# Second feed-forward stage: TensorE's steps of the state-space preparation one group later; output matrices signed on GpSimd

## The chip, the cores and the metric

One core of a Trainium2 chip runs the whole program, two transformer blocks over 256 tokens of width 1024, in one launch. The metric is the device time of that launch in microseconds, the median of several runs. Lower is better.

## The reference, cut to what matters

The change lies where the first block's second feed-forward stage runs and the second block's state-space mixer is prepared:

```python
x = x + 0.5 * _swiglu(_rms_norm(x, ffn2_norm), ffn2_w1, ffn2_w3, ffn2_w2)   # D_FF = 2816
...
dt = exp(log_dt);  mag = exp(lam_re * dt);  ang = lam_im * dt
lb = mag * (cos(ang) + i sin(ang))          # 32 groups x 64 complex states
f  = (lb - 1) / lam;  bb = f * b            # input matrices
bu = einsum('bsgh,gph->sbgp', u, bb)
st = associative_scan(st[t] = lb * st[t-1] + bu[t])
y  = Re(c) . Re(st) - Im(c) . Im(st) + d_skip * u
```

The kernel works the scan in chunks of four tokens. For that it needs, from the parameters alone: powers of `lb` (`pw`), the input matrices times these powers (`ws`), their transposes (`bx`), the products of `c` with them for the tokens inside a chunk (`kt`), `c` times the powers with a sign on the imaginary half (`cy`), and tables of `exp(i ang t)` (`E`) and of decays (`R4`). None of it depends on the tokens, so it is computed beside the second feed-forward stage.

## The kernel before

The two feed-forward stages are one function, `ffn` (L418). It runs over 11 groups of 256 hidden units. For each group it takes four weight blocks of 512 KB from a stream (`W.next()`), makes 2 x 48 matmuls `hT` (three for each product, for the high and low parts of both sides), a SiLU and a product on ScalarE and VectorE, and then `second`, 24 matmuls `yacc` with two more weight blocks for the group before. Each weight block `w` is split by `wsplit` (L294): ScalarE writes the high part `whi` (L301), VectorE the low part `wlo` (L316; the first of a stage at L308, one of them on GpSimd). `whi` and `wlo` have four buffers each.

`s5_prep` (L806) returns the preparation as steps for `ffn`'s `hooks`: a step of group g is written out ahead of that group's own work. `params` (group 0) and `powers` (1) make the small tables in `s5z`; `inputs` (2) makes `ws` on GpSimd, four rounds of six operations of 128x512 and eight copies; `kernels(o)` (groups 4 to 7, o = 0 to 3) has the TensorE step: eight transposes `bxp` (L896) and eight small products `k` (L350) that read `ws[o]`, then two ScalarE copies to `bx` (L897) and ten to `kt` (L907). `kernels(0)` also clears the two halves of `kt` on GpSimd (L890, L891). `outputs` (8) makes the four `cy` from products `ctmp` on GpSimd, 24 operations, and four sign changes on VectorE (L919). `tables` (9) makes `E` and `R4`.

Nothing runs in the order in which it is written. A scheduler takes the instructions by priority, the earlier written ahead of the later, as their inputs and buffers come free by its own estimate of times, and fixes one order for each engine; on the chip each engine then works its list strictly in order and waits by semaphores. `after(i, j)` (L322) orders i behind j on that list; `pinned` (L339) keeps a chain of matmuls in the order written, in stages where it is on (it is off in the feed-forward stages). Buffers: `Q` has 9 slots of 512 columns, which the SiLU results also use; `M` has two tags, `m` with 6 slots (`wide=False`: `bc`, `kt`, two of the `cy`) and `r3` with 13 (`wide=True`).

Of the kernel before, what the change touches and what calls it, by code (L numbers as in the profile page):

```python
# [12 lines left out]
OP = mybir.AluOpType  # L13
# [36 lines left out]
def transformer_kernel(ctx: ExitStack, tc: tile.TileContext, A, out, stop=None):  # L50
# [50 lines left out]
    def Q(shape, dt=F32, name="q"):  # L101
        return tl(qpool, "q", 512, shape, dt, name)
# [234 lines left out]
    def pinned(i):  # L337

        if "pin" in cur:  # L339
            if cur["pin"] is not None:  # L340
                after(i, cur["pin"])
            cur["pin"] = i

    def mm3(o, lh, ll, rh, rl, start, stop):
        pinned(PE.matmul(o, lh, rh, start=start, stop=False))  # L345
        pinned(PE.matmul(o, lh, rl, start=False, stop=False))  # L346
        pinned(PE.matmul(o, ll, rh, start=False, stop=stop))  # L347

    def mm(o, l, r, start=True, stop=True, **kw):
        pinned(PE.matmul(o, l, r, start=start, stop=stop, **kw))  # L350
# [454 lines left out]

    def s5_prep(pr):  # L806

        z = M([28, 16], name="s5z", wide=True)
        lre, lim = vec[:, V_LRE:V_LRE + 16], vec[:, V_LIM:V_LIM + 16]
        dt, mag, ang, sn, cs, half = (z[:, n, :] for n in range(6))  # L810
        t = [z[:, n, :] for n in range(6, 10)]
# [2 lines left out]
        pw[0] = (lbr, lbi)  # L814
        r4 = z[:, 23, :]
        un = [(z[:, 24, :], z[:, 25, :]), (z[:, 26, :], z[:, 27, :])]

        def bcast(q):
            return q[:, :, None].to_broadcast([P, 16, 32])
# [37 lines left out]
        def powers():  # L857
            cmul(*pw[1], lbr, lbi, lbr, lbi, t, G)
            cmul(*pw[2], *pw[1], lbr, lbi, t, G)
            cmul(*pw[3], *pw[1], *pw[1], t, G)  # L860
            G.tensor_tensor(r4, mag, mag, op=OP.mult)
            G.tensor_tensor(r4, r4, r4, op=OP.mult)
            cmul(*un[0], cs, sn, cs, sn, t, G)
            cmul(*un[1], *un[0], *un[0], t, G)

        def inputs():

            pr["ws"] = [M([2, 4, 4, 32], name="ws", wide=True) for _ in range(4)]
            b = pr["bc"][0]
            for n in range(4):  # L870
                tmp = [Q([16, 32], name="wtmp") for _ in range(2)]
                cur_ = H([2, 16, 32], name="wcur")
                cur_ = [cur_[:, 0], cur_[:, 1]]
                if n == 0:
                    cmul(cur_[0], cur_[1], b[:, 0], b[:, 1], bcast(fr), bcast(fi), tmp, G)
                else:
                    cmul(cur_[0], cur_[1], last[0], last[1], bcast(lbr), bcast(lbi), tmp, G)
                for o in range(4):
                    for ri in range(2):
                        G.tensor_copy(pr["ws"][o][:, ri, :, 3 - n, :], cur_[ri][:, 4 * o:4 * o + 4, :])  # L880
                last = cur_

        def kernels(o):
            def f():
                if o == 0:
                    pr["cim"] = Q([16, 32], name="cim")
                    V.tensor_scalar(pr["cim"], pr["bc"][1][:, 1], -1.0, None, op0=OP.mult)
                    pr["bx"] = [M([2, 4, P], name="bx", wide=True) for _ in range(4)]
                    pr["kt"] = [M([16, 2, 32], name="kt", wide=False) for _ in range(2)]
                    G.memset(pr["kt"][0], 0.0)  # L890
                    G.memset(pr["kt"][1], 0.0)  # L891
                wp = pr["ws"][o].rearrange("p r t j h -> p r t (j h)")
                for ri in range(2):
                    p = PT([4, P], name="bxp")
                    for i in range(4):
                        PE.transpose(p[:, i, :], wp[:, ri, i, :], ident)  # L896
                    S.copy(pr["bx"][o][:, ri], p)  # L897
                pk = PT([4, 32], name="k")
                for i in range(4):
                    tt = 4 * o + i  # L900
                    mm(pk[:, i, :], wp[:, 0, i, :], pr["bc"][1][:, 0, tt, :], start=True, stop=False)
                    mm(pk[:, i, :], wp[:, 1, i, :], pr["cim"][:, tt, :], start=False, stop=True)

                for j in range(4):
                    for jj in range(j + 1):
                        src = 3 - (j - jj)
                        S.copy(pr["kt"][j // 2][jj * 32:(jj + 1) * 32, 4 * o:4 * o + 4, j % 2, :],  # L907
                               pk[src * 32:(src + 1) * 32, :, :])
            return f

        def outputs():
            pr["cy"] = [M([2, 16, 32], name="cy", wide=n < 2) for n in range(4)]
            c = pr["bc"][1]
            for n in range(4):
                tmp = M([2, 16, 32], name="ctmp", wide=True)
                tmp = [tmp[:, 0], tmp[:, 1]]
                cy = pr["cy"][n]
                cmul(cy[:, 0], cy[:, 1], c[:, 0], c[:, 1], bcast(pw[n][0]), bcast(pw[n][1]), tmp, G)
                V.tensor_scalar(cy[:, 1], cy[:, 1], -1.0, None, op0=OP.mult)  # L919

        def tables():

# [6 lines left out]
            for k in range(6):  # L929
# [9 lines left out]
            V.tensor_copy(R4, r4[:, :, None].to_broadcast([P, 16, 64]))  # L939
            V.memset(R4[:, :, 0:1], 0.0)  # L940

        return {0: [params], 1: [powers], 2: [inputs], 4: [kernels(0)], 5: [kernels(1)], 6: [kernels(2)],
                7: [kernels(3)], 8: [outputs], 9: [tables]}

    def s5_pool(x, pr, before):
        for i in range(2):
# [806 lines left out]
```

## Time and profile before

| | |
|---|---|
| median of 3 runs | 1308.74 us (1304.94 to 1309.45) |
| the profiled execution | 1304.89 us |
| its span, first to last instruction | 1302.7 us |
| TensorE (PE) busy | 1241.5 us, 95% |
| VectorE (DVE), ScalarE (ACT), GpSimd (POOL) busy | 607.7, 514.9, 269.3 us |
| mean granted clock of TensorE | 0.972 of full speed |
| second feed-forward stage | about 339 to 545 us |

The profile is one execution. Its parts used here: the busy time of the engines; the same in stretches of the span, with the clock that TensorE was granted (1.00 is 2.4 GHz, 0.50 is 1.2 GHz); each engine's instructions in order of time, with the idle time before one in brackets and what ended it; and the instructions on one tile. Times are microseconds from the start of the span. A TensorE row's duration is that of a pipelined matmul; the distance between two starts is what one costs.

### The profile page before, as it was taken

Reading aid. Unit: us, or ns where it says so; the run is one execution under the profiler, and the core shown is the slowest. Engines: PE = TensorE matmul, PEld = TensorE weight load, DVE = VectorE, ACT = ScalarE, POOL = GpSimd, SP = SyncE. Lnnn points to the kernel's source line nnn. Section 1 sums busy time; section 2 is a strip of 40 time slices with the busy share of each in tenths; the row PEclk is TensorE's granted clock in tenths of the full one; section 3 lists DMA queues with packets and bytes.
Section 4 is the critical chain, followed back from the end, with each engine's and each line's share of the span. In section 5 each row is a group of like instructions: output and inputs, shape, how many; then the busy total and the mean of one; then the engine's idle time right before and its main releaser. Section 6 shows DMA issues by size and latency. Waiting matters only on the chain. (4 is left out here: it accounts for less than half of the span.)

```text
span 1302.7 us, 19644 instructions
## 1 busy us (share of the span) xinstructions
PE 1241.5 (95%) x7726; PEld 906.6 (70%) x7726; DVE 607.7 (47%) x975; ACT 514.9 (40%) x774; POOL 269.3 (21%) x318
## 2 busy tenths in 40 slices
PE   8999999999999999998999997997999999997996
PEld 7999997887898999897635453445988734454433
DVE  6445548886664645477512123115755514114113
ACT  5444445575444554435421131114677422122111
POOL 4000001002499547213101220002311101220001
PEclk9999999999898999999999998998999899998998
DMA  9765565435454556536899997999835698998995
GB/s 342 232 188 184 181 191 178 131 130 169 138 179 128 176 152 199 165 128 229 325 395 384 386 385 276 395 398 369 329 112 180 218 373 302 383 389 311 358 393 216
DMA packets 175273, 335.36 MB, mean 257 GB/s; under 512 B 10337, under 2 KB 72305, under 8 KB 175170
## 3 DMA queue, kind: packets, MB, share of 16 engines
q1 hardware_dynamic: 173696, 330.34, 71.8%
q0 software_dynamic: 896, 2.98, 0.6%
q8 instruction: 64, 1.05, 0.3%
q10 hardware_dynamic: 578, 0.67, 0.2%
q14 instruction: 39, 0.32, 0.1%
HBM read 332.91 MB, written 1.05 MB: 256 GB/s over the span
## 5 line engine op out<-in xcount | busy, mean ns | idle before, releaser
L316 DVE TENSOR_TENSOR wlo<-w,whi 128x1024 fp32r<-128x1024 f32 x200 | 266.2, 1338 | 208.5 <-ACT whi L301 205.8
L301 ACT ACTIVATE whi<-w 128x1024 fp32r<-128x1024 f32 x234 | 246.4, 1059 | 247.3 <-PE hT L346 118.8
L350 PE MATMUL h<-w,xg 128*64 128x512 f32 x1024 | 225.6, 594 | 0.5
L345 PE MATMUL hT<-xTh,whi 128*128 128x256 f32 x704 | 202.1, 287 | 0.1
L346 PE MATMUL hT<-xTl,whi 128*128 128x256 f32 x704 | 201.3, 286 | 0.4 <-DVE xTl L334 0.3
L347 PE MATMUL hT<-xTh,wlo 128*128 128x256 f32 x704 | 200.8, 286 | 0.0
L350 PEld LDWEIGHTS h<-w,xg 128*64 128x64 f32 x1024 | 72.3, 137 | 137.8 <-issue 132.1
L345 PEld LDWEIGHTS hT<-xTh,whi 128*128 128x128 f32 x704 | 137.3, 195 | 1.5 <-ACT xTh L332 0.5
L346 PEld LDWEIGHTS hT<-xTl,whi 128*128 128x128 f32 x704 | 137.1, 195 | 1.4 <-DVE xTl L334 0.8
L347 PEld LDWEIGHTS hT<-xTh,wlo 128*128 128x128 f32 x704 | 136.9, 195 | 0.0
L350 PE MATMUL ey<-w,ehTs 128*64 128x512 f32 x512 | 114.2, 593 | 0.4
L335 DVE SCALAR_TENSOR_TENSOR yl<-ey,sgate,yh 128x512 fp32r<-128x512 f32 x32 | 24.0, 749 | 180.1 <-ACT yh L332 179.0
L332 ACT ACTIVATE yh<-ey,sgate 128x512 fp32r<-128x512 f32 x32 | 22.0, 688 | 167.6 <-PE ey L350 127.3
L350 PEld LDWEIGHTS ey<-w,ehTs 128*64 128x64 f32 x512 | 38.6, 137 | 70.8 <-issue 62.8
L316 POOL TENSOR_TENSOR wlo<-w,whi 128x1024 fp32r<-128x1024 f32 x16 | 37.7, 2382 | 222.2 <-ACT whi L301 142.4
L345 PE MATMUL tr<-xTh,whi 128*128 128x256 f32 x256 | 73.9, 289 | 0.4 <-ACT xTh L332 0.4
L346 PE MATMUL tr<-xTl,whi 128*128 128x256 f32 x256 | 73.2, 286 | 0.3 <-DVE xTl L334 0.3
L347 PE MATMUL tr<-xTh,wlo 128*128 128x256 f32 x256 | 72.6, 284 | 0.0
L346 PE MATMUL yacc<-wlo,hh 128*128 128x512 f32 x176 | 68.7, 391 | 0.0
L345 PE MATMUL yacc<-whi,hh 128*128 128x512 f32 x176 | 68.7, 390 | 0.0
L347 PE MATMUL yacc<-whi,hl 128*128 128x512 f32 x176 | 68.6, 390 | 0.0
L357 POOL TENSOR_TENSOR brs<-rp,cm 128x1 f32<-128x1 f32 x8 | 4.4, 550 | 299.3 <-DVE rp L356 297.4
(444 smaller groups left out, 2138.1 us busy)
## 6 DMA issues: line engine op xcount, KB each, us to landing
w<-in_moe_w SPq DMA_DIRECT2D x384, 512.0 KB, 10.2
w<-in_ffn_w SPq DMA_DIRECT2D x132, 512.0 KB, 4.3
w<-in_w_in SPq DMA_DIRECT2D x28, 512.0 KB, 3.9
w<-in_sb_qkv SPq DMA_DIRECT2D x24, 512.0 KB, 10.5
w<-in_ple_gate SPq DMA_DIRECT2D x16, 512.0 KB, 9.0
w<-in_w_out SPq DMA_DIRECT2D x8, 512.0 KB, 3.2
w<-in_ab_w_in SPq DMA_DIRECT2D x8, 512.0 KB, 4.4
w<-in_ab_w_out SPq DMA_DIRECT2D x8, 512.0 KB, 4.1
```

Of the source, the lines that this page charges most:

```text
L301: a = S.activation(hi, t, AF.Copy)
L316: i = eng.tensor_tensor(lo, t, fb(hi), op=OP.subtract)
L332: cur["act"] = S.activation(hi, src, AF.Copy if isinstance(scale, float) else AF.Identity, scale=scale)
L335: return V.scalar_tensor_tensor(lo, src, scale, fb(hi), op0=OP.mult, op1=OP.subtract)
L345: pinned(PE.matmul(o, lh, rh, start=start, stop=False))
L346: pinned(PE.matmul(o, lh, rl, start=False, stop=False))
L347: pinned(PE.matmul(o, ll, rh, start=False, stop=stop))
L350: pinned(PE.matmul(o, l, r, start=start, stop=stop, **kw))
L357: cur["pow"] = G.tensor_tensor(o, t, cm05[:, :n], op=OP.pow)
```

## The change

Four edits, all in the preparation:

- The hook table: `kernels(0)` to `kernels(3)` go from groups 4 to 7 to groups 5 to 8, `outputs` from 8 to 3, `tables` from 9 to 8.
- The transposes `bxp` are ordered behind the matmul that `mm3` wrote last (`cur["mm3"]`), which is the last `yacc` of the group before.
- `outputs` no longer subtracts and then changes a sign on VectorE. `powers` makes negated powers `neg` on GpSimd (eight operations of 128x16), and each half of a `cy` is two products and a sum.
- The products `wtmp` of `inputs` lie in `M` (tag `r3`), no longer in `Q`.

```diff
--- before.py
+++ after.py
@@ -344,7 +344,8 @@
     def mm3(o, lh, ll, rh, rl, start, stop):
         pinned(PE.matmul(o, lh, rh, start=start, stop=False))
         pinned(PE.matmul(o, lh, rl, start=False, stop=False))
-        pinned(PE.matmul(o, ll, rh, start=False, stop=stop))
+        cur["mm3"] = PE.matmul(o, ll, rh, start=False, stop=stop)
+        pinned(cur["mm3"])
 
     def mm(o, l, r, start=True, stop=True, **kw):
         pinned(PE.matmul(o, l, r, start=start, stop=stop, **kw))
@@ -805,7 +806,7 @@
 
     def s5_prep(pr):
 
-        z = M([28, 16], name="s5z", wide=True)
+        z = M([36, 16], name="s5z", wide=True)
         lre, lim = vec[:, V_LRE:V_LRE + 16], vec[:, V_LIM:V_LIM + 16]
         dt, mag, ang, sn, cs, half = (z[:, n, :] for n in range(6))
         t = [z[:, n, :] for n in range(6, 10)]
@@ -814,6 +815,8 @@
         pw[0] = (lbr, lbi)
         r4 = z[:, 23, :]
         un = [(z[:, 24, :], z[:, 25, :]), (z[:, 26, :], z[:, 27, :])]
+
+        neg = [(z[:, 28 + 2 * n, :], z[:, 29 + 2 * n, :]) for n in range(4)]
 
         def bcast(q):
             return q[:, :, None].to_broadcast([P, 16, 32])
@@ -862,13 +865,17 @@
             G.tensor_tensor(r4, r4, r4, op=OP.mult)
             cmul(*un[0], cs, sn, cs, sn, t, G)
             cmul(*un[1], *un[0], *un[0], t, G)
+            for q, w in zip(neg, pw):
+                for ri in range(2):
+                    G.tensor_scalar(q[ri], w[ri], -1.0, None, op0=OP.mult)
 
         def inputs():
 
             pr["ws"] = [M([2, 4, 4, 32], name="ws", wide=True) for _ in range(4)]
             b = pr["bc"][0]
             for n in range(4):
-                tmp = [Q([16, 32], name="wtmp") for _ in range(2)]
+                tmp = M([2, 16, 32], name="wtmp", wide=True)
+                tmp = [tmp[:, 0], tmp[:, 1]]
                 cur_ = H([2, 16, 32], name="wcur")
                 cur_ = [cur_[:, 0], cur_[:, 1]]
                 if n == 0:
@@ -893,7 +900,7 @@
                 for ri in range(2):
                     p = PT([4, P], name="bxp")
                     for i in range(4):
-                        PE.transpose(p[:, i, :], wp[:, ri, i, :], ident)
+                        after(PE.transpose(p[:, i, :], wp[:, ri, i, :], ident), cur["mm3"])
                     S.copy(pr["bx"][o][:, ri], p)
                 pk = PT([4, 32], name="k")
                 for i in range(4):
@@ -915,8 +922,12 @@
                 tmp = M([2, 16, 32], name="ctmp", wide=True)
                 tmp = [tmp[:, 0], tmp[:, 1]]
                 cy = pr["cy"][n]
-                cmul(cy[:, 0], cy[:, 1], c[:, 0], c[:, 1], bcast(pw[n][0]), bcast(pw[n][1]), tmp, G)
-                V.tensor_scalar(cy[:, 1], cy[:, 1], -1.0, None, op0=OP.mult)
+
+                w, q = [bcast(v) for v in pw[n]], [bcast(v) for v in neg[n]]
+                for ri, (a, b) in enumerate(((w[0], q[1]), (q[1], q[0]))):
+                    G.tensor_tensor(tmp[0], c[:, 0], a, op=OP.mult)
+                    G.tensor_tensor(tmp[1], c[:, 1], b, op=OP.mult)
+                    G.tensor_tensor(cy[:, ri], tmp[0], tmp[1], op=OP.add)
 
         def tables():
 
@@ -939,8 +950,8 @@
             V.tensor_copy(R4, r4[:, :, None].to_broadcast([P, 16, 64]))
             V.memset(R4[:, :, 0:1], 0.0)
 
-        return {0: [params], 1: [powers], 2: [inputs], 4: [kernels(0)], 5: [kernels(1)], 6: [kernels(2)],
-                7: [kernels(3)], 8: [outputs], 9: [tables]}
+        return {0: [params], 1: [powers], 2: [inputs], 3: [outputs], 5: [kernels(0)], 6: [kernels(1)], 7: [kernels(2)],
+                8: [kernels(3), tables]}
 
     def s5_pool(x, pr, before):
         for i in range(2):
```

What this does to the order on TensorE: the last products of a group (`yacc`; the number behind `whi` is its buffer: `whi_4125` holds block 123, the second one of `second` after group 3's `hT`) and preparation step 0, before.

```order
L346 MATMUL yacc_3391<-wlo_4126,hh_3948 128x512
L347 MATMUL yacc_3391<-whi_4125,hl_3949 128x512
L896 MATMUL bxp_4163<-identr_104,ws_3751 128x128 x4
L896 MATMUL bxp_4169<-identr_104,ws_3751 128x128 x4
L350 MATMUL k_4175<-bc_3393,ws_3751 128x32
L350 MATMUL k_4175<-cim_4153,ws_3751 128x32
```

And with the change (`whi_4326` holds block 129, the one after group 4's `hT`).

```order
L346 MATMUL yacc_3391<-wlo_4327,hh_4149 128x512
L347 MATMUL yacc_3391<-whi_4326,hl_4150 128x512
L903 MATMUL bxp_4364<-identr_104,ws_3759 128x128 x4
L903 MATMUL bxp_4370<-identr_104,ws_3759 128x128 x4
L351 MATMUL k_4376<-bc_3393,ws_3759 128x32
L351 MATMUL k_4376<-cim_4354,ws_3759 128x32
```

The step has moved behind the next group's products; steps 1 to 3 take the places one further on in the same way, and the rest of TensorE's list is the same.

GpSimd's list where the two clears of `kt` stand, before: ahead of the stage's first `wlo` and of the two roots of its norm (`rstd`). In brackets are the semaphores an instruction waits for.

```order
L824 DMA bc_3392<-in_bc 128x1024
L824 DMA bc_3393<-in_bc 128x1024 [waits DMASW0_49,PE_49]
L890 MEMSET kt_4159 128x1024 [waits PE_49]
L891 MEMSET kt_4160 128x1024 [waits PE_49]
L308 TENSOR_TENSOR wlo_3428<-w102_3089,whi_3427 128x1024 [waits DMAHW3_49,DVE_49,Activation_49]
L407 TENSOR_TENSOR rstd_3339<-rstd_3339,cm05_99 128x1 [waits DVE_49]
L407 TENSOR_TENSOR rstd_3349<-rstd_3349,cm05_99 128x1 [waits DVE_49]
```

And with the change: among the last operations of `outputs`.

```order
L930 TENSOR_TENSOR cy_3994<-ctmp_4010 128x512 [waits Pool_49]
L930 TENSOR_TENSOR cy_3995<-ctmp_4017 128x512 [waits Pool_49]
L897 MEMSET kt_4360 128x1024 [waits PE_49]
L928 TENSOR_TENSOR ctmp_4017<-bc_3393,s5z_3331 128x512 [waits Pool_49]
L929 TENSOR_TENSOR ctmp_4017<-bc_3393,s5z_3331 128x512
L898 MEMSET kt_4361 128x1024 [waits PE_49]
L930 TENSOR_TENSOR cy_3995<-ctmp_4017 128x512 [waits Pool_49]
```

The clears have moved from ahead of the stage to behind `ws` and most of `cy`: 19 of the 24 operations on `ctmp` and `cy` stand between the last `ws` copy and the first clear.

ScalarE's list at preparation step 0, before: the casts `whi` of the weights, the copies to `bx` and `kt`, and the next casts.

```order
L301 ACTIVATE whi_4263<-w127_3958 128x1024 [waits DMAHW4_49,PE_49,Activation_49]
L897 COPY bx_4155<-bxp_4163 128x512 [waits DMASW5_49,PE_49]
L897 COPY bx_4155<-bxp_4169 128x512 [waits PE_49]
L907 COPY kt_4159<-k_4175 32x4x32 [waits PE_49]
L907 COPY kt_4159<-k_4175 32x4x32 x2
L907 COPY kt_4160<-k_4175 32x4x32 x7
L301 ACTIVATE whi_4325<-w128_3988 128x1024 [waits DMAHW5_49,PE_49,Activation_49]
```

And with the change.

```order
L301 ACTIVATE whi_4464<-w133_4159 128x1024 [waits DMAHW2_49,PE_49,Activation_49]
L904 COPY bx_4356<-bxp_4364 128x512 [waits PE_49,Pool_49]
L904 COPY bx_4356<-bxp_4370 128x512 [waits PE_49]
L914 COPY kt_4360<-k_4376 32x4x32 [waits PE_49,Pool_49]
L914 COPY kt_4360<-k_4376 32x4x32 x2
L914 COPY kt_4361<-k_4376 32x4x32 [waits Pool_49]
L914 COPY kt_4361<-k_4376 32x4x32 x6
L301 ACTIVATE whi_4526<-w134_4189 128x1024 [waits DMAHW3_49,PE_49,Activation_49]
```

The first copy into each half of `kt` now also waits for GpSimd (`Pool_49`), and the casts of blocks 134 and following stand behind these copies, where it was block 128 and following before.

## Rows read from the trace of the kernel before

**Rows 1.** The page, busy time: us (share of the span) xinstructions, all engines.

```profile
PE 1241.5 (95%) x7726; PEld 906.6 (70%) x7726; DVE 607.7 (47%) x975; ACT 514.9 (40%) x774; POOL 269.3 (21%) x318
```

**Rows 2.** Stages around 405 us: busy us (xinstructions) by engine, clock, DMA share, GB/s.

```profile
405.00:414.00 9.00, 5.84 (x26) 5.25 (x26) 3.63 (x4) 2.35 (x4) 9.00 (x13) 0.63 0.38 117
414.00:418.00 4.00, 4.00 (x22) 4.00 (x22) 0.00 (x0) 2.46 (x10) 3.92 (x4) 0.55 0.40 125
418.00:432.00 14.00, 14.00 (x100) 13.12 (x99) 9.06 (x6) 6.15 (x7) 14.00 (x11) 1.00 0.35 115
```

**Rows 3.** TensorE's timeline, group 3 to 4: start, us, line, output<-inputs [idle before].

```profile
404.81 0.39 PE L347 MATMUL yacc<-whi,hl 128*128 128x512 f32 x1
...
407.32 1.12 PE L896 MATMUL bxp<-identr,ws 128*128 128x128 f32 x4 [2.12 <-POOL ws L880]
...
410.38 0.47 PE L350 MATMUL k<-bc,ws 128*128 128x32 f32 x2
...
417.43 0.35 PE L347 MATMUL hT<-xTh,wlo 128*128 128x256 f32 x1
```

**Rows 4.** TensorE's timeline, preparation step 1 and the group behind it.

```profile
432.45 1.04 PE L896 MATMUL bxp<-identr,ws 128*128 128x128 f32 x8
...
435.03 0.37 PE L345 MATMUL hT<-xTh,whi 128*128 128x256 f32 x1
...
446.63 0.40 PE L345 MATMUL yacc<-whi,hh 128*128 128x512 f32 x1
...
452.10 1.03 PE L896 MATMUL bxp<-identr,ws 128*128 128x128 f32 x8
```

**Rows 5.** GpSimd's timeline, from the `kt` clears to the stage's end.

```profile
323.31 0.95 POOL L890 MEMSET kt<- 128x1024 f32 x1 [4.27 <-PE oacc L346]
...
345.43 0.22 POOL L800 TENSOR_TENSOR s5z<-s5z 128x16 f32<-128x16 f32 x1 [8.48 <-DVE s5z L854]
...
359.21 1.05 POOL L799 TENSOR_TENSOR wtmp<-bc,s5z 128x512 f32<-128x512 f32 x1
...
397.96 1.70 POOL L880 COPY ws<-wcur 128x128 f32<-128x128 f32 x7
...
408.43 4.34 POOL L880 COPY ws<-wcur 128x128 f32<-128x128 f32 x7
...
417.12 1.05 POOL L802 TENSOR_TENSOR ctmp<-bc,s5z 128x512 f32<-128x512 f32 x1
...
420.14 1.30 POOL L804 TENSOR_TENSOR cy<-ctmp 128x512 f32<-128x512 f32 x1
...
423.63 2.03 POOL L799 TENSOR_TENSOR ctmp<-bc,s5z 128x512 f32<-128x512 f32 x1
...
545.16 4.74 POOL L308 TENSOR_TENSOR wlo<-w,whi 128x1024 fp32r<-128x1024 f32 x2 [31.87 <-ACT whi L301]
```

**Rows 6.** Tile `kt`: duration min/median/max and waits; ScalarE's timeline at 405.28.

```profile
L907 ACT COPY kt<-k x40: 255/258/262, 413.9 to 477.0; 32x128 f32<-32x128 f32 x40
...
  PE k L350: 4.2, 4
...
405.28 1.06 ACT L301 ACTIVATE whi<-w 128x1024 fp32r<-128x1024 f32 x1 [0.30 <-PE yacc L347]
```

**Rows 7.** VectorE's timeline: an undisturbed `wlo`; first and last pair beside `inputs`.

```profile
342.01 1.22 DVE L308 TENSOR_TENSOR wlo<-w,whi 128x1024 fp32r<-128x1024 f32 x1
...
359.63 3.70 DVE L316 TENSOR_TENSOR wlo<-w,whi 128x1024 fp32r<-128x1024 f32 x2 [2.18 <-ACT whi L301]
...
409.62 2.53 DVE L316 TENSOR_TENSOR wlo<-w,whi 128x1024 fp32r<-128x1024 f32 x2
```

**Rows 8.** Busy time and clock behind the pause at the stage's start.

```profile
339.00:345.00 6.00, 5.96 (x26) 5.33 (x25) 5.97 (x15) 0.73 (x2) 0.00 (x0) 0.51 0.28 89
```

**Rows 9.** Busy time while GpSimd runs `outputs` (21 operations).

```profile
412.80:443.25 30.45, 30.45 (x217) 29.44 (x218) 15.48 (x10) 16.44 (x33) 28.70 (x21) 0.92 0.43 134
```

**Rows 10.** Waits between 395 and 425 us: us in total, times, longest.

```profile
DVE hl L334 <- POOL wcur L804: 4.8, 1, 4.8
```

## The prediction

> **What bounds the kernel now.** I read the page's head first: TensorE is busy for 1241.5 of 1302.7 us, the other engines for less than half of it [rows 1]. So a change pays only where TensorE stands still or runs at its lower clock, and costs only where it makes TensorE do so. Next the busy time and granted clock stage by stage around the lines that change, the second feed-forward stage: TensorE is busy for only 5.84 of 9 us and at clock 0.63 from 405 to 414 us, full but at 0.55 from 414 to 418, and from 418 on full at 1.00 [rows 2]; the other stretches of the stage are like the last. TensorE's timeline says what stands there: the last product of a group starts at 404.81 (the 24 of a group start 0.23 apart: 5.47 us, below; so its successor was due at 405.04), the transposes `bxp` of preparation step 0 start at 407.32, after a wait for GpSimd's `ws`; work is dense again from 410.38, at the lower of the two clock levels (1.2 of 2.4 GHz) until 417.43 [rows 3].
>
> The same step without a wait is step 1: it starts at 432.45, `hT` follows at 435.03, `yacc` at 446.63, and step 2 stands at 452.10 [rows 4]. That gives the units: step 2.58 us, two `hT` blocks 11.60, `yacc` 5.47, a group with a step 19.65, one without 17.07.
>
> **What the change takes away.** From 405.04 to 432.45 are 27.41 us for a step and a group that take 19.65 elsewhere: the wait and the half clock behind it cost 7.76 us. After the change step 0 stands one group later, at 405.04 + 17.07 = 422.1. GpSimd's last `ws` copy ends at 412.77 now [rows 5]; with the new queue it starts 0.4 earlier, does 5 fewer short operations before that point (33 and 6 negations for 44; 13.8 us for 44, so 0.31 each: -1.5), two `ctmp` products more (+2.0), and meets two VectorE subtractions more (+2.1, below), since VectorE no longer stands behind `wtmp`: about 414.9. That is 7 us ahead of 422.1, so the old wait is gone: **-7.76 us**. The order bound to the last product changes nothing by itself: the transposes stood behind it before as well.
>
> **What the change adds: a wait on ScalarE.** `kernels(0)` also clears `kt`, and ScalarE's ten copies into it need that. Before, the clears ran from 323.31, long ahead [rows 5], and the 40 copies waited for TensorE's `k` alone [rows 6]. In the new order the clears stand on GpSimd behind the `ws` copies and 19 and 21 of the 24 operations of `outputs`. ScalarE works its queue in order, and behind the `kt` copies stand the `whi` of all later weights. So when does GpSimd reach the second clear?
>
> An undisturbed product takes 1.05 us, and three fill 417.12 to 420.14, so one starts 1.01 after the other; an undisturbed sum takes 1.30; a clear 0.95 [rows 5]. Operations that meet a VectorE `wlo` take about one more: a product 2.03 [rows 5]. The price of one comes from the whole of `inputs`: 359.21 to 412.74 is 53.5 us; undisturbed, its four rounds need 4 x (4 x 1.01 + 2 x 1.30 + 8 x 0.24) = 34.3 (seven copies ran in 1.70); VectorE did 18 `wlo` in that time (first and last pair: [rows 7]); 19.2 / 18 = 1.07 us each. From 414.9 on: a sum (1.3), four products and two sums (6.6), then again four and two, and again, that is 12 x 1.01 + 7 x 1.30 = 21.2 us to the first clear, plus four `wlo` (two of group 4, and the pair whose `whi` are cast when the group ends, the second as at 405.28 before [rows 6]) at 1.07 = 4.3. First clear 440.4 to 441.4, two products, second clear done at **444.3**. After about 424 no `wlo` is left to disturb it, since ScalarE itself stands.
>
> ScalarE reaches the copies when `k` ends, near 424.7. Three go into the first half at 441.4, seven into the second from 444.3, at 0.26 each [rows 6]: 446.1. Then comes `whi` of the next block (1.06 [rows 6]): 447.2, and its `wlo` (1.22 where nothing disturbs it, as at 342.01 [rows 7]): 448.4. Who waits? TensorE has the split weights of both `hT` of group 5, cast ahead of the copies, so it runs 11.60 us past 424.7, to 436.3; then the first `yacc` needs the late `whi`, the second the late `wlo`. Standing time 448.4 - 436.3 = 12.1, less the one product in between (0.3): 11.8. After such a pause it comes back at the lower clock: dense work from 410.38 ran at half until 417.43, 7.05 us; behind the pause at the stage's start it was 0.51 over 339 to 345 [rows 3, 8]. At half speed 7.05 us do the work of 3.5: 3.5 us lost. Together **+15.3**.
>
> **Sum**: 15.3 - 7.76 = +7.5 us. Bounds of the added term: if GpSimd ran `outputs` without any hold-up from 412.74 on, second clear at 412.74 + 21.2 + 0.95 + 2.02 + 0.95 = 437.9, 6.4 us sooner: +1.1. If all 21 operations took the mean of before (28.7 us for the 21 that ran from 412.8 to 443.25 [rows 9]), 414.9 + 28.7 + 1.9 = 445.5: +8.7; with the half clock as long as from the pause's first matmuls at 407.32 to 417.43 (10.1 us, 1.5 us dearer [rows 3]), +10.2. I take the middle, since GpSimd meets four `wlo` there, not none, and not one for every second operation.
>
> What [rows 5] show is one of two engines held up while the other is at the SBUF. The Trainium skill ("SBUF — State Buffer", section "SBUF: two separate sides") says that VectorE and GpSimd share a pair of ports as an exclusive lock, held for a whole instruction, also by a VectorE operation with two SBUF inputs against a GpSimd operation that reads SBUF. By that rule a `wlo` costs its whole 1.22 us where the rows give 1.07; six of them (the two more and the four) would put the clear 0.9 us later and the sum at +8.4. The trace agrees in kind (2.03 for 1.05), and a little less in size.
>
> **Edits with no price.** Four sign operations on VectorE go; that engine's queue is not what TensorE waits for at their place, so they give nothing back. The eight negations on GpSimd are in the sum as far as they stand ahead of the `ws` copies; the first two now stand ahead of the stage's first GpSimd `wlo`, where the two clears of 0.95 us stood [rows 5]. `wtmp` in another pool frees VectorE of a wait of 4.8 us that TensorE did not feel beyond the stall counted above [rows 10]. No DMA is added; the one for `poolw` on GpSimd's queue waits for the same TensorE product. Steps 1 to 3 find `ws` and `kt` ready. GpSimd's `tables` end about 32 us before its next work at 545.16 [rows 5]; after the change one small clear in them waits for TensorE's step 2, which moves a group later (some 20 us), so they still end ahead of that work, which moves back with TensorE too. The weight ring refills in time: DMA is 0.35 to 0.40 busy here [rows 2].
>
> **Rivals.** (a) *It works as it reads, faster.* The clears come in time, TensorE never stands: -7.76, 1301.0 us. The point: the second clear done by 436.3 - 1.2 - 1.1 - 1.8 = 432.2, 12 us before my 444.3. For it speaks that the sum of undisturbed GpSimd times alone would allow it (19 us of hold-up lie in `inputs`); against it, that 25 us of undisturbed work stand between the last `ws` copy and the end of the second clear, and 17 us between that copy and 432.2. 10%. (b) *Smaller stall*, second clear at about 438 to 443: +1 to +6.2; the lower half of my own mechanism. (c) *A stall elsewhere*: `ws` later than 422.1 (it has 7 us), or `tables` late for the scan at the state-space stage (it has some 30 us); each would add to the forecast, 4% together. (d) *The change does not do what it says*: the order shows TensorE's step a group later and the signs gone from VectorE, so this has no chance worth naming.
>
> **How the numbers follow.** The profiled execution took 1304.9 us (span 1302.7), the median of the runs is 1308.7; against its own time the sum gives 1312.4, against the median **1316.2**, which I predict. About 0.5% (6.5 us) is what a measurement of this kernel can tell from no change, so the threshold lies at 1315.3, just below. My mechanism has 85%, centred on +7.5 with bounds +1.1 and +10.2 and run-to-run differences of a few us: some 53% above +6.5, 32% within. With (a), (c), and 1% for what I don't see: faster 0.11, same 0.34, slower 0.55. The range leaves out (a) and the lowest part of (b): 1308 to 1321.
>
> **What would show it.** In the profile after: `bxp` near 422 with no wait for `ws`, and the half-clock stretch at 408 to 417 gone; the two `kt` clears on GpSimd near 440 to 445; the first `kt` copy on ScalarE waiting some 16 us for a GpSimd clear; a TensorE gap of about 12 us between the second `hT` and `yacc` near 436 to 448, then 0.41-us matmuls for some 7 us. It is wrong if the clears end before 432 or if TensorE bridges the pause with other work.

## The result, and the profile after

The changed kernel takes 1317.39 us, the median of five runs (1312.46 to 1318.25), against 1308.03 us (1304.94 to 1309.45) for the kernel before on the same chip: a ratio of 1.0074, 95% interval 1.0054 to 1.0094. It is slower by some 9 us where 7.5 were predicted. The mechanism that I named is nevertheless not the one that acted. Times are compared among fast runs only; in experiment 1 three of four runs are counted as slow, since they lie more than 1.5% above the fourth, so no ratio is formed there.

The profiled execution (span 1315.7 us) tells where to look. The page's busy line of the changed kernel, and two of its groups (busy us, mean ns of one, idle time just before and what ended most of it):

```profile
PE 1241.7 (94%) x7726; PEld 904.3 (69%) x7726; DVE 634.2 (48%) x971; ACT 514.3 (39%) x774; POOL 260.4 (20%) x326
...
L316 DVE TENSOR_TENSOR wlo<-w,whi 128x1024 fp32r<-128x1024 f32 x200 | 293.1, 1473 | 199.9 <-ACT whi L301 195.6
...
L346 PE MATMUL yacc<-wlo,hh 128*128 128x512 f32 x176 | 69.9, 397 | 15.4 <-DVE wlo L316 15.4
```

Against [rows 1] TensorE does the same work. VectorE has four instructions fewer and is busy 26.5 us longer, all of it at `wlo`: the same 200 subtractions took 266.2 us before. And TensorE waited 15.4 us for a `wlo` at a `yacc` product, a group of products that waited 0.0 us before.

TensorE's timeline around that wait, and the step that was moved:

```profile
403.91 0.28 PE L345 MATMUL hT<-xTh,whi 128*128 128x256 f32 x1
...
418.11 0.39 PE L345 MATMUL yacc<-whi,hh 128*128 128x512 f32 x1
433.94 0.80 PE L346 MATMUL yacc<-wlo,hh 128*128 128x512 f32 x1 [15.44 <-DVE wlo L316]
...
434.96 0.63 PE L345 MATMUL yacc<-whi,hh 128*128 128x512 f32 x1
435.39 0.63 PE L346 MATMUL yacc<-wlo,hh 128*128 128x512 f32 x1
...
441.27 0.40 PE L347 MATMUL yacc<-whi,hl 128*128 128x512 f32 x1
441.51 1.04 PE L903 MATMUL bxp<-identr,ws 128*128 128x128 f32 x8
```

Group 4 starts at 403.91 and goes straight on from group 3: the old wait for `ws` [rows 3] is gone. Undisturbed, step 0 would follow at 403.91 + 17.07 = 420.98. It starts at 441.51, waiting for nothing then. Between lie 20.5 us: two `hT` waits for `wlo` (2.2), the wait of 15.4, and the half clock behind it (the rows at 434.96 and 435.39: one product costs 0.43 instead of 0.23; 23 products took 7.57 instead of 5.24: 2.3); 0.6 is not placed. In the kernel before, the transposes at this place (those of step 1) start at 432.45 [rows 4]; without step 0 ahead of them (2.58) that would be 429.87, so 441.51 is 11.6 us late. That is 20.5, less the 7.76 removed, less 1.1 by which group 4 began earlier (403.91 for 405.04). The whole stage is 11.6 us longer; the rest of the span's 13.0 lies elsewhere, and the five runs scatter by 6.

What VectorE and GpSimd did in that time (start, us, line, output<-inputs, count, [idle before]). VectorE, three of its subtractions:

```profile
398.17 7.46 DVE L316 TENSOR_TENSOR wlo<-w,whi 128x1024 fp32r<-128x1024 f32 x1 [2.26 <-ACT whi L301]
...
412.13 21.76 DVE L316 TENSOR_TENSOR wlo<-w,whi 128x1024 fp32r<-128x1024 f32 x1 [0.86 <-ACT whi L301]
433.81 2.06 DVE L316 TENSOR_TENSOR wlo<-w,whi 128x1024 fp32r<-128x1024 f32 x1
```

GpSimd, the end of `inputs` and `outputs`:

```profile
404.49 1.28 POOL L887 COPY ws<-wcur 128x128 f32<-128x128 f32 x1
...
412.10 1.29 POOL L930 TENSOR_TENSOR cy<-ctmp 128x512 f32<-128x512 f32 x1
413.35 2.05 POOL L928 TENSOR_TENSOR ctmp<-bc,s5z 128x512 f32<-128x512 f32 x2
415.37 2.05 POOL L929 TENSOR_TENSOR ctmp<-bc,s5z 128x512 f32<-128x512 f32 x2
417.38 2.51 POOL L930 TENSOR_TENSOR cy<-ctmp 128x512 f32<-128x512 f32 x2
...
430.33 2.47 POOL L930 TENSOR_TENSOR cy<-ctmp 128x512 f32<-128x512 f32 x2
432.75 0.94 POOL L897 MEMSET kt<- 128x1024 f32 x1
433.67 1.13 POOL L928 TENSOR_TENSOR ctmp<-bc,s5z 128x512 f32<-128x512 f32 x1
434.76 2.02 POOL L929 TENSOR_TENSOR ctmp<-bc,s5z 128x512 f32<-128x512 f32 x1
436.73 0.95 POOL L898 MEMSET kt<- 128x1024 f32 x1
```

One subtraction "ran" 21.76 us, where an undisturbed one takes 1.22 [rows 7]. Its row counts waiting as busy. All that time GpSimd ran 19 products and sums back to back at their undisturbed pace (1.01 for a product). The subtraction ends at 433.89, 1.14 us after the first clear of `kt` starts: it was let in there. The one at 398.17 ends at 405.63, 1.14 after the `ws` copy at 404.49 starts. In the kernel before the two engines took turns in `outputs`, at one more us for each operation of GpSimd that met one ([rows 5], 2.03 at 423.63). The clears, last, were in time for ScalarE:

```profile
444.35 2.68 ACT L914 COPY kt<-k 32x128 f32<-32x128 f32 x10 [0.57 <-PE k L351]
```

So the loss that I had put on ScalarE and `kt` came from VectorE and `wlo` instead. The questions: why does VectorE not get its turn here, and is my mechanism absent or only hidden?

### The profile page after: what moved, and what is told of

The parts are those of the page before. It is cut to its first block, busy times and chain, and to the rows that moved or that the text cites. A ratio compares the mean times of both kernels' runs of the same rounds, so it can differ in the third digit from the quotient of the medians.

```text
span 1315.7 us, 19648 instructions
## 1 busy us (share of the span) xinstructions
PE 1241.7 (94%) x7726; PEld 904.3 (69%) x7726; DVE 634.2 (48%) x971; ACT 514.3 (39%) x774; POOL 260.4 (20%) x326
## 3 DMA queue, kind: packets, MB, share of 16 engines
q8 instruction: 64, 1.05, 0.3%
HBM read 332.91 MB, written 1.05 MB: 254 GB/s over the span
## 5 line engine op out<-in xcount | busy, mean ns | idle before, releaser
L316 DVE TENSOR_TENSOR wlo<-w,whi 128x1024 fp32r<-128x1024 f32 x200 | 293.1, 1473 | 199.9 <-ACT whi L301 195.6
L346 PE MATMUL yacc<-wlo,hh 128*128 128x512 f32 x176 | 69.9, 397 | 15.4 <-DVE wlo L316 15.4
L1361 DVE TENSOR_TENSOR es<-es,h 128x512 f32<-128x512 f32 x16 | 11.0, 687 | 113.6 <-PE h L351 87.0
```

The costliest lines, as they stand in the source:

```text
L316: i = eng.tensor_tensor(lo, t, fb(hi), op=OP.subtract)
L1361: V.tensor_tensor(s, s, h3, op=OP.mult)
```

## The experiments

The theories: (T1) it is the order of `outputs`, whose operations run back to back; (T2) it is the late clears, as predicted; (T3) it is `wtmp` in `M`, which changes `inputs` and the order in it; (T4) the clears matter as instructions that leave the two engines in another state, wherever they stand; and, after experiments 1 to 4, (T5) VectorE gets turns when GpSimd has lately had to wait. The kernel before was timed again beside them: 1305.93 us with experiments 1 to 4, 1303.53 with 5 to 7, 1304.46 with 11 and 12 (7 to 11 runs each). A ratio is against the one of its own group.

**1. The clears early.** The two clears go to the head of `powers`.

```diff
         def powers():
+            pr["kt"] = [M([16, 2, 32], name="kt", wide=False) for _ in range(2)]
+            G.memset(pr["kt"][0], 0.0)
+            G.memset(pr["kt"][1], 0.0)
```

> The changed kernel with one thing else: the two clears of kt are issued at the head of powers, ahead of GpSimd's long queue, so that ScalarE's kt copies can wait for nothing. Theory T1 (the new order of GpSimd's products and sums, back to back with no operation that needs the result of the one just before, leaves VectorE's wlo no turn): as after, TensorE stands about 15 us from 418 on for a wlo of over 15 us, 1316 to 1319 us. Theory T2 (that of the prediction: ScalarE waits for late clears): stall gone, 1300 to 1302. Theory T4 (a clear on GpSimd is what lets VectorE have its turns again, as at 432.75 in after): since the clears now run ahead of the stage, wlo gets in at each operation, 1300 to 1303. Theory T3 (something that inputs and powers do ahead of outputs, such as wtmp in the M pool): as after, 1316 to 1319.

Measured: 1317.57, 1318.0, 1317.73 and 1297.76 us; since one of four lies 20 us off, no ratio is given. In the profiled run (1317.57) the clears run at 324.69 and 325.58, and VectorE is still shut out, for the same 21.76 us as in the changed kernel:

```profile
413.36 21.76 DVE L316 TENSOR_TENSOR wlo<-w,whi 128x1024 fp32r<-128x1024 f32 x1 [0.85 <-ACT whi L301]
```

It ends at 435.12, 1.13 after the next thing on GpSimd that is no long product or sum, a 128x16 operation on `s5z` at 433.99. TensorE waits for `wlo` as there (15.4 us), so T2 and T4 fall as the cause of the loss in this run. The run of 1297.76 says that the same program can also be 20 us faster; there is no trace of it, so what went otherwise in it is not shown.

**2. Product, product, sum.** Each sum is ordered behind its own two products, so that it should wait for the second.

```diff
+                    i = G.tensor_tensor(tmp[0], c[:, 0], a, op=OP.mult)
+                    if "chain" in cur:
+                        after(i, cur["chain"])
+                    j = G.tensor_tensor(tmp[1], c[:, 1], b, op=OP.mult)
+                    after(j, i)
+                    cur["chain"] = G.tensor_tensor(cy[:, ri], tmp[0], tmp[1], op=OP.add)
```

> The changed kernel with the operations of outputs in a fixed order on GpSimd: product, product, sum of the same pair, so that each sum waits for the product right before it; nothing is taken away and the clears of kt stay late. T1: each wait of a sum gives VectorE a turn, no wlo above 5 us inside outputs, TensorE's stand of 15 us gone: 1300 to 1304. T2: 1316 to 1319. T3 and T4: 1316 to 1319.

Measured: 1309.79 us (7 runs, 1307.72 to 1311.89), ratio 1.0034 (1.0019 to 1.0049). The long subtraction in `outputs` is gone, and the wait that I had predicted is there. VectorE, GpSimd and ScalarE in time, then the longest waits (us in total, times, longest):

```profile
413.11 2.35 DVE L316 TENSOR_TENSOR wlo<-w,whi 128x1024 fp32r<-128x1024 f32 x1 [0.85 <-ACT whi L301]
...
414.34 1.20 POOL L803 TENSOR_TENSOR s5z<-s5z 128x16 f32<-128x16 f32 x1
415.50 1.20 POOL L804 TENSOR_TENSOR s5z<-s5z 128x16 f32<-128x16 f32 x1
...
441.86 0.95 POOL L897 MEMSET kt<- 128x1024 f32 x1
...
444.76 0.95 POOL L898 MEMSET kt<- 128x1024 f32 x1
...
442.84 0.80 ACT L914 COPY kt<-k 32x128 f32<-32x128 f32 x3 [16.01 <-POOL kt L897]
445.75 1.86 ACT L914 COPY kt<-k 32x128 f32<-32x128 f32 x7 [2.10 <-POOL kt L898]
...
PE yacc L345 <- ACT whi L301: 9.8, 1, 9.8
```

So there are two mechanisms, and the first hides the second: with VectorE shut out, TensorE comes late to `bxp`, and the clears are done by then. What gave VectorE its turns is less clean than the edit: the new order also put two short operations of `powers` behind the first sum (414.34 and 415.50), and the first two turns came there (413.11 + 2.35 = 415.46, 1.12 after 414.34). The first pause of 0.08 us on GpSimd stands only at 427.39. So the order decides; that it is the sum's wait, this run does not show.

**3. The old form of the sums at the new place.** Subtraction as before; the sign of the second half of `cy` is left out, so `cy` has the wrong sign there.

```diff
-                w, q = [bcast(v) for v in pw[n]], [bcast(v) for v in neg[n]]
-                for ri, (a, b) in enumerate(((w[0], q[1]), (q[1], q[0]))):
...
+                cmul(cy[:, 0], cy[:, 1], c[:, 0], c[:, 1], bcast(pw[n][0]), bcast(pw[n][1]), tmp, G)
```

> The changed kernel with outputs written as before (two products and a difference, two products and a sum), at its new place; the sign of the second half of cy is left out altogether (neither GpSimd nor VectorE makes it). GpSimd's order of products is then that of before, one position earlier. T1 in its strict form (it is the order of the new form): 1300 to 1304 with wlo of about 2 us in outputs, as before at 421 to 434. T2, T3, T4: 1316 to 1319 with a wlo of over 15 us.

Measured: 1316.4 us (5 runs, 1311.33 to 1318.49), ratio 1.0069 (1.0046 to 1.0091); the first subtraction beside `outputs` again 21.76 us. The arithmetic on GpSimd is not the cause; what is left is the place.

**4. `outputs` late.** Hooks as changed, but `outputs` at group 8 and `tables` at 9, as before; the clears then come early by themselves.

```diff
-        return {0: [params], 1: [powers], 2: [inputs], 3: [outputs], 5: [kernels(0)], 6: [kernels(1)], 7: [kernels(2)],
-                8: [kernels(3), tables]}
+        return {0: [params], 1: [powers], 2: [inputs], 5: [kernels(0)], 6: [kernels(1)], 7: [kernels(2)],
+                8: [kernels(3), outputs], 9: [tables]}
```

> The changed kernel with outputs called at group 8 and tables at group 9 as before; its new form, the steps of TensorE one group later and everything else as changed. The clears of kt then run ahead of the stage and no ctmp product stands between the operations of inputs, but outputs follows the last ws copy in the same back-to-back order as in after. T1: as after, 1314 to 1319, wlo of over 15 us inside outputs. T2 and T4: 1300 to 1303. T3: as after.

Measured: 1296.36 us (4 runs, 1296.12 to 1299.53), ratio 0.9936 (0.9913 to 0.9959), faster than any of the theories had it. TensorE has no wait in this stretch, and step 0 stands where the prediction's first part puts it; GpSimd at the start of `outputs`:

```profile
420.59 1.03 PE L903 MATMUL bxp<-identr,ws 128*128 128x128 f32 x8
...
412.93 1.04 POOL L928 TENSOR_TENSOR ctmp<-bc,s5z 128x512 f32<-128x512 f32 x1
413.94 1.04 POOL L929 TENSOR_TENSOR ctmp<-bc,s5z 128x512 f32<-128x512 f32 x1
415.06 2.18 POOL L930 TENSOR_TENSOR cy<-ctmp 128x512 f32<-128x512 f32 x1
```

`outputs` itself still runs beside group 4, since GpSimd is free then; yet VectorE gets its turns (no subtraction beside `outputs` takes over 2.3 us). What differs is in the last rows: the sum waits for its product (413.94 + 1.04 = 414.98, start 415.06), as in the kernel before at 414.87 (413.74 + 1.05 = 414.79). In the changed kernel no sum waits: both products of the first pair ran beside `inputs` (399.22 and 401.48), and each later sum has another operation between itself and its second product. Two short operations on `s5z` stand ahead of the products here as well (412.58 and 412.76); the third probe below tells the two apart. T3, with `wtmp` in `M` here too, doesn't hold as stated, nor T1 in the form that back-to-back long operations alone decide: most of these stand back to back too.

**5. One short operation.** Clears early, and one product of the first pair put behind the last `ws` copy, so that the first sum waits.

```diff
+                    if n == 0 and ri == 0:
+                        after(j, cur["ws_last"])
+                        cur["first_sum"] = k
+                    else:
+                        after(i, cur["first_sum"])
+                        after(j, cur["first_sum"])
```

> e1_clears_early with one change of order: the second product of the first pair of outputs stands behind the last ws copy, then one short s5z operation, then the sum that needs that product; the other 21 operations of outputs follow in the order of after. Theory T5 (new, read from before, after, e1 and e4: VectorE gets a turn between two long GpSimd operations only if GpSimd has stood waiting a short while ago; in before 10 of 10 such places with at most 12 operations since GpSimd's last idle gap gave VectorE the turn, in after and e1 none of more than 20 with 64 or more): the sum's wait right ahead of the long row puts GpSimd back, every wlo in outputs stays under 3 us: 1296 to 1301 us. Rival T1 (back-to-back independent operations never give a turn, whatever came ahead): wlo gets in at the short operation and the next one is shut out for over 10 us: 1305 to 1318.

Measured: 1295.69 us (4 runs, 1295.4 to 1300.08), ratio 0.9935 (0.9918 to 0.9953), no `wlo` there beyond 2.3 us. As T5 expects, but the proof isn't clean: VectorE had its turns already in the last round of `inputs`, ahead of the edit's place.

**6. Both remedies.** The edits of 1 and 2 together.

> e2_chain and e1_clears_early together: outputs in the order product, product, sum, and the clears of kt ahead of the stage. In the trace of e2 ScalarE's first kt copy stood 16.0 us for the late clear, as the prediction had it, once VectorE was not shut out. If these two are all there is: both gone, no TensorE stand over 3 us between 400 and 450, 1296 to 1300 us, as e4. If something else is lost in the order of e2: 1305 to 1311.

Measured: 1295.14 us (4 runs, 1294.63 to 1298.63), ratio 0.9939 (0.9916 to 0.9962), no wait of TensorE over 0.8 us there. The two mechanisms account for the whole loss. From 2 to 6 only the clears move. Experiment 2 is 3.86 us above the kernel before that was timed with it (1305.93), experiment 6 is 8.39 below its own (1303.53): 12.3 us is what the late clears cost where nothing hides it.

**7. `wtmp` back in `Q`.** The third theory by itself.

```diff
-                tmp = M([2, 16, 32], name="wtmp", wide=True)
-                tmp = [tmp[:, 0], tmp[:, 1]]
+                tmp = [Q([16, 32], name="wtmp") for _ in range(2)]
```

> The changed kernel with one part undone: wtmp is two tiles of the Q pool again, as before; powers then ends ahead of inputs, and ctmp products and sums of outputs stand between the operations of inputs. T5: from the second round of inputs on no operation needs the result of the one just before, so GpSimd runs some 50 operations without a gap by 412 and VectorE is shut out in outputs as in after: 1310 to 1319. T3 (the wtmp tile in the M pool is what shuts VectorE out): no wlo over 5 us, and ScalarE's wait for the late clears shows as in e2: 1306 to 1311.

Measured: 1313.35 us (4 runs, 1312.6 to 1314.1), ratio 1.0071 (1.0053 to 1.0089). T3 falls. Both mechanisms show, at other places; VectorE, TensorE, GpSimd, ScalarE:

```profile
405.70 8.67 DVE L316 TENSOR_TENSOR wlo<-w,whi 128x1024 fp32r<-128x1024 f32 x1 [8.51 <-ACT whi L301]
...
414.43 0.58 PE L347 MATMUL hT<-xTh,wlo 128*128 128x256 f32 x1 [8.19 <-DVE wlo L316]
...
413.15 1.37 POOL L886 COPY ws<-wcur 128x128 f32<-128x128 f32 x1
...
422.95 2.16 POOL L929 TENSOR_TENSOR cy<-ctmp 128x512 f32<-128x512 f32 x1
...
444.63 0.80 ACT L913 COPY kt<-k 32x128 f32<-32x128 f32 x3 [9.04 <-POOL kt L896]
```

VectorE is shut out in the last round of `inputs` until the `ws` copy at 413.15 (405.70 + 8.67 = 414.37, 1.22 later). The 21 us in `outputs` that I expected do not come: the sum at 422.95 waited for its product there.

**8 to 10. The dispute by itself.** A program of its own, with nothing of the reference: GpSimd runs a row of n + 28 independent products (128x512) after standing idle; when product n, counted from 0, is done (so n + 1 are), VectorE starts three subtractions of the size of a `wlo`.

```diff
+STAGES = (4, 12, 20, 28, 40, 64)
...
+        for k in range(n + 28):
+            i = product(dst, k)
...
+        for j in range(3):
+            v = V.tensor_tensor(wlo[j], x[0], x[1], op=OP.subtract)
```

> A kernel of its own that does none of the reference's work: six stages; in each GpSimd, after an idle gap, does n + 28 independent products of 128x512 as in outputs (n = 4, 12, 20, 28, 40, 64), and VectorE, once product n is done, does three subtractions of 128x1024 from two SBUF tiles as wlo. T5: the first subtraction of the stages 4 and 12 takes 1.3 to 2.4 us, that of stage 64 about 27 us (shut out until the products end), with a change-over in between. T1: all six about 27 us. If products alone never shut VectorE out (it needs what the kernel has around them): all six 1.3 to 2.4 us.

Measured, VectorE's three subtractions together, for n = 4 and then 12 (20, 28, 40 and 64 are the same 30.39):

```profile
10.78 5.95 DVE L52 TENSOR_TENSOR wlo<-x,x 128x1024 f32<-128x1024 f32 x3
...
54.52 30.39 DVE L52 TENSOR_TENSOR wlo<-x,x 128x1024 f32<-128x1024 f32 x3
```

With n = 4 they take turns; with n = 12 or more VectorE's first subtraction stands until GpSimd's row is over (27 more products of 1.01; it takes 28.1 us). The same with n = 30, 4, 8, 6, 10, 5, 7, 30, 3 in this sequence:

> m1_probe with other numbers of products ahead of VectorE's three subtractions, not in rising order: n = 30, 4, 8, 6, 10, 5, 7, 30, 3; it does none of the reference's work. If the length of the row since GpSimd's idle gap decides: short rows 1.3 to 2.4 us per subtraction, long rows 27 us for the first, with one change-over between 5 and 13 products, wherever the stage stands. If it was the first stage of m1 alone that differed (its first eight products wait for nothing, those of later stages each wait for an operation eight places ahead): all nine stages but the first shut out, also n = 4 and 3, and the first, n = 30, perhaps as well.

Measured: 30.37 and 30.36 us at both n = 30, and 5.95 or 5.96 for all the others, with n = 10 the longest:

```profile
192.28 5.95 DVE L52 TENSOR_TENSOR wlo<-x,x 128x1024 f32<-128x1024 f32 x3
```

So the change comes between n = 10 and n = 12, that is between 11 and 13 products done since GpSimd last stood idle, whatever ran earlier. Third, n = 20 and one other operation at product n + 5: none, a product that waits for the one ahead of it, a 128x16 product, a 128x128 copy, a clear, a sum that needn't wait.

> m1_probe with n = 20 in each of six stages; five operations behind product n stands one other operation, and 22 products behind that: nothing special (one more independent product), a product that reads the result of the operation just before it, a 128x16 product, a 128x128 copy, a clear of 128x512, a sum of two results of three and four operations ago; it does none of the reference's work. T5 and the kernel's traces (VectorE got in at ws copies, short s5z operations, a kt clear, and behind the wait of a sum, but not at cy sums whose operands were ready): the first subtraction takes about 27 us in the stages with nothing special and with the ready sum, and 5 to 8 us with the waiting product, the short product, the copy and the clear. If only a wait of GpSimd lets VectorE in: 5 to 8 us with the waiting product alone.

Measured, in this sequence:

```profile
26.90 30.36 DVE L68 TENSOR_TENSOR wlo<-x,x 128x1024 f32<-128x1024 f32 x3
...
79.16 9.18 DVE L68 TENSOR_TENSOR wlo<-x,x 128x1024 f32<-128x1024 f32 x3
...
131.12 29.39 DVE L68 TENSOR_TENSOR wlo<-x,x 128x1024 f32<-128x1024 f32 x3
...
182.40 29.51 DVE L68 TENSOR_TENSOR wlo<-x,x 128x1024 f32<-128x1024 f32 x3
...
233.82 8.97 DVE L68 TENSOR_TENSOR wlo<-x,x 128x1024 f32<-128x1024 f32 x3
...
284.55 30.58 DVE L68 TENSOR_TENSOR wlo<-x,x 128x1024 f32<-128x1024 f32 x3
```

A wait or a clear ends the shutting out, for the two subtractions that follow too (2.28 and 2.06 us; 2.06 and 2.06). A short operation or a copy lets a single subtraction in; the next stands again, as the first two of the third row by themselves show:

```profile
131.12 5.00 DVE L68 TENSOR_TENSOR wlo<-x,x 128x1024 f32<-128x1024 f32 x1
136.03 23.34 DVE L68 TENSOR_TENSOR wlo<-x,x 128x1024 f32<-128x1024 f32 x1
```

That is what the kernels show: the `ws` copies of the changed kernel let one in each (404.49) and VectorE is shut out again behind them; the clear at 432.75 ends it.

**11. The rule put to use in the kernel.** The two clears stand right behind the first pair's sums in `outputs`: as a remedy for both mechanisms at once, were the probe right.

```diff
+                    k = G.tensor_tensor(cy[:, ri], tmp[0], tmp[1], op=OP.add)
+                if n == 0:
+                    pr["kt"] = [M([16, 2, 32], name="kt", wide=False) for _ in range(2)]
+                    for q in pr["kt"]:
+                        after(G.memset(q, 0.0), k)
```

> The changed kernel with one thing else: the two clears of kt stand on GpSimd right behind the second sum of the first of the four parts of outputs, seven long operations behind the last ws copy, where the probe m3 says a clear ends the shut-out for good (first subtraction 5.0 us, the next two 2.06 us each). GpSimd reaches them at about 418.6 by the pitch of after. If the probe's rule holds in the kernel: the wlo that asks at 412 ends near 420 instead of 433.9 (8 us long), the next ones take about 2 us, TensorE stands some 1 to 4 us instead of 15.4, the kt copies find their clears done: 1297 to 1302 us. If a clear lets one wlo in and the row shuts the next one out again: a second wlo of about 8 us and 1303 to 1310. If the clears change nothing: 1316 to 1319.

Measured: 1299.15 us (4 runs, 1297.09 to 1301.31), ratio 0.9949 (0.9932 to 0.9965). VectorE's first subtraction, and GpSimd:

```profile
412.11 7.62 DVE L316 TENSOR_TENSOR wlo<-w,whi 128x1024 fp32r<-128x1024 f32 x1 [0.86 <-ACT whi L301]
...
418.59 1.83 POOL L931 MEMSET kt<- 128x1024 f32 x2
...
421.98 4.02 POOL L925 TENSOR_TENSOR ctmp<-bc,s5z 128x512 f32<-128x512 f32 x2
...
437.06 3.52 POOL L927 TENSOR_TENSOR cy<-ctmp 128x512 f32<-128x512 f32 x2
```

It is shut out until the first clear (412.11 + 7.62 = 419.73, 1.14 after 418.59), and behind it the engines take turns (two products in 4.02), still at the end of the row (two sums in 3.52 at 437.06, where two that meet nothing take 2.51). TensorE's longest wait for a `wlo` there is 1.4 us, and the `kt` copies wait for no clear.

**12. The kernel of experiment 4 again**, with more runs, as the version that beats both.

> e4_outputs_late a second time, unchanged, to know the size of its gain better: the prediction's price of the old wait alone is 7.76 us, and the stage's start comes back to the full clock some 1 us sooner in after than in before, so 7.5 to 10 us below the kernel before (ratio 0.9925 to 0.9943), as the 9.6 us of the first time.

Measured: 1296.59 us (6 runs, 1294.41 to 1300.69), ratio 0.9932 (0.9919 to 0.9945): 7.9 us faster than before.

## Why the prediction was right in size and wrong in cause

- **What is removed: right.** -7.76 was counted; experiments 4, 6 and 12, with neither mechanism in the way, are faster by 7.9 to 9.6 us, perhaps 1.1 of it told below. `ws` is ready at 412.1 in the changed kernel (414.9 predicted), and `bxp` stands at 420.59 in experiment 4 (422.1 predicted). The 414.9 itself had a miscount: in the 13.8 us of the kernel before the trace has 38 short operations, not 44, so 39 are one more and not five fewer; by the sum's other terms `ws` would have come near 417, still ahead of `bxp`.
- **The step that failed** is "Operations that meet a VectorE `wlo` take about one more": it took for granted that GpSimd gives way, as in [rows 5]. In the changed kernel it gives way nowhere between 412.10 and 432.75. Its second clear is done at 437.68, which is the 437.9 that I had as the bound without any hold-up, and VectorE pays instead: 21.76 us for one subtraction. TensorE has the low parts for group 4's `hT`, but not those of the `second` behind it, so it stops at 418.5, ahead of `bxp`, where I had it stop at 436, in the group behind.
- **ScalarE's wait on `kt`: a real mechanism, but hidden.** In the changed kernel the copies wait 0.57 us, for `k`. In experiment 2, where VectorE gets its turns, the clears end at 442.81 and 445.71 (441.4 and 444.3 predicted), the first copy waits 16.0 us (some 16), TensorE stands for 9.8 (11.8). Experiments 2 and 6 price it at 12.3 us, half clock included; I had 15.3.
- **So the size came out by chance.** Either mechanism is worth more than the gain: VectorE's stand 15.4 + 2.2 + 2.3, ScalarE's 12.3. They don't add up, since the first delays what the second would meet. Experiment 1, which mends only the second, keeps the whole first one in its trace; experiment 2, which mends only the first, still ends above the kernel before.
- **The half clock: 2.3 us, 3.5 predicted.** The work behind the wait costs 0.43 for a product until 438.38 (4.4 us, not 7.05).
- **Not foreseen: 1.1 us at the head of the stage**, where TensorE's granted clock over 339 to 345 is 0.72 (0.51 in [rows 8]). No run looked into it; since experiment 6, with the change in it, has 0.51 there and experiment 4 has 0.72, it need not come from the change.

```profile
339.00:345.00 6.00, 5.89 (x34) 5.16 (x33) 5.97 (x14) 0.93 (x2) 0.00 (x0) 0.72 0.26 79
...
422.00:438.00 16.00, 4.06 (x10) 3.20 (x11) 16.00 (x4) 0.00 (x0) 16.00 (x15) 0.50 0.17 45
```

These are windows of the changed kernel, columns as in [rows 2]; the second is the loss in one line: VectorE and GpSimd busy for 16 of 16 us, TensorE for 4, ScalarE for none.

- **The weighed rule.** The Trainium skill ("SBUF — State Buffer", section "SBUF: two separate sides") has the shared ports go to whichever of the two starts first, for the whole instruction. The trace agrees that one stands while the other works. But the wait that mattered was not one instruction long: VectorE stood through 19 of GpSimd's in a row.

**What stays open.** Why the chip keeps VectorE out, by the count of operations or by something that goes with it, is not settled: I know only the change between 11 and 13 products done and what ends it. In experiment 5 VectorE got turns that a bare count since GpSimd's last wait doesn't explain, and in experiment 11 they go on to the thirteenth product or sum behind the clears, after several of the thirteen had met a subtraction. Whether being held up by VectorE counts for GpSimd as a wait was not tried. The run of 1297.76 in experiment 1 is not explained.

## What to carry to other kernels

Before work is packed more densely on GpSimd beside VectorE operations that TensorE needs, look whether GpSimd ever waits or clears something in that stretch; a wait of 0.08 us may be what lets VectorE in. Read the longest single instruction of a line, not only its mean: two subtractions of 21.76 and 7.46 us among 200 moved the mean only from 1338 to 1473 ns and the engine's busy time by 4%. And when an added delay is masked by another, undo them one at a time and together: either alone may seem worth nothing.

## What the runs showed of the hardware

- GpSimd and VectorE take turns, at about 1 us for each operation that meets another, when VectorE asks after at most 11 products of 128x512 since GpSimd last stood idle; from 13 on, a subtraction of 128x1024 that starts then stands until GpSimd's row ends (28.1 us in the probe, all of it shown as VectorE's busy time).
- A GpSimd operation that waits for the one ahead of it, or a clear, brings the turns back; a 128x16 product or a 128x128 copy lets in one subtraction (5.00 us, then 23.34); a sum that needn't wait lets in none.
- One program (experiment 1) took 1317.6 to 1318.0 us in three runs and 1297.76 in the fourth; only one of the three has a trace, and in it VectorE was shut out.
